# Ordering the taps of a depthwise convolution around a triangular inverse on VectorE

## The chip, the core and the metric

The kernel is one program on one core of a Trainium2 chip. The metric is the device time of one execution in microseconds, the median of several runs. Engines are named as the profile names them: PE (TensorE matmul), PEld (its weight loads), DVE (VectorE), ACT (ScalarE), POOL (GpSimd), SP (SyncE).

## The reference, cut to what matters

The reference runs three transformer-like blocks one after the other on one sequence of 512 tokens with 1024 channels, in fp32. Only the mixing layer of the second block is touched here. It has two branches that meet in one output projection:

```python
y_a = rwkv7_time_mix(...)          # 16 heads of 64; a recurrence over 512 tokens:
#   sa = S @ a_t;  S = S * w_t + sa b_t^T + v_t k_t^T;  y_t = S @ r_t
y_b = conformer_conv(conv_in, ...) # glu = u[:1024] * sigmoid(u[1024:]);
#   z = depthwise causal convolution of glu, 31 taps, 1024 channels, + bias; layer norm; silu
merged = concat([y_a, y_b]) * gates
x = x + gt_m * (merged @ w_out)
```

## The kernel before

Activations lie channel-major, 128 channels by 512 tokens a tile. Each large product is split into three matmuls of a high and a low part (`mm3`, lines 123 to 125); the weights come by DMA on SP's queue and are split by `wsplit` into `whi` (line 117, ACT) and `wlo` (line 118, DVE or POOL).

**The recurrence.** The time mix works on eight pairs of heads, p = 0 to 7, one after the other. For each pair:

- `rwkv_prep` projects r, k and v (matmul, then `shift`, line 1029 on DVE: the tiles `xs_k`, `xs_r`, `xs_v`), normalises k (`kksq` on ACT, the small matmul `ps_kn` on PE, line 1086), makes the products of a chunk with itself (`ps_M`, then `MLR` on DVE, line 1119) and writes the 32 by 32 diagonal blocks to DRAM (`dram_L`).
- `rwkv_invert` reads them back as `uL` (a DMA on ACT's queue), sets the diagonal to one on POOL (line 1161) and inverts the blocks on DVE: 35 small instructions that depend on one another, first a copy of 128x256 into `uM` (line 1177), then multiplies and sums (lines 1171, 1172, 1181 to 1187). The last sum is remembered as `self.inv_last`. The result goes by DRAM into `DT`, and PE finishes it (`ps_D`, `ps_T`, `ps_X`).
- `rwkv_steps` goes through eight chunks of 64 tokens, each a chain PE, DVE and ACT (`zV`, lines 1251 and 1252), PE (`ps_u`), ACT, PE (`ps_s`), DVE (`S`, line 1261). Pair p needs the inverse of p.

**The convolution.** `conv_tiles` makes one or two of the eight tiles of the convolution: a matmul, a gate (`glu`, line 1301 on DVE), a first tap on ACT (line 1303), and then 30 taps on DVE (line 1305), each of which reads and writes the whole tile `z[i]`, so that the taps of one tile form a chain. It is called between the pairs with low priority ("filler"), in the order

```python
order = ["c01", "c12", "c31 g02", "c42", "g22", "c62 g41", ...]
```

where "c12" is `conv_tiles` of two tiles from tile 1 on. List entry 0 is emitted after the inverse of pair 0, entry p + 1 after the inverse of pair p + 1. So the taps of tile 0 are emitted behind inverse 0, those of tiles 1 and 2 behind inverse 1, of tile 3 behind inverse 2, of tiles 4 and 5 behind inverse 3, of tiles 6 and 7 behind inverse 5. Tap 1 of each tile may not be issued before `inv_last` of the inverse that it was emitted behind.

**The order on an engine.** The code is traced once, and a planner fixes at build time in which order each engine issues its instructions: by priority, and by its own notion of when operands are ready. On the chip each engine keeps that order; an instruction that waits holds back all behind it. `issue_after(ins, earlier)` adds an edge for the planner alone, without a semaphore: `ins` stands behind `earlier`.

Of the kernel before, what the change touches and what calls it, by code (L numbers as in the profile page):

```python
# [328 lines left out]
class Block1:  # L329
# [5 lines left out]
    def attend(self, scores, bias, vt, po):  # L335
# [3 lines left out]
        for q0 in (0, 2):  # L339
            PTs = []  # L340
            for e in range(2):
                PT = self.app.tile([128, NB, T // 2], F32, tag="PT", name="PT", bufs=4)
                PTs.append(PT)
                for qb in (q0, q0 + 1):
# [3 lines left out]
                    den = self.sp.tile([128, 1], F32, tag="den", name="den", bufs=6)  # L348
                    p = self.app.tile([128, T], F32, tag="P", name="P", bufs=3)
                    if bias is not None:  # L350
# [240 lines left out]
    def layer1(self):  # L591
# [11 lines left out]
        with ExitStack() as st:  # L603
# [11 lines left out]
            for g0 in range(0, 8, 4):  # L615
                ws = app.tile([128, NB, T // NB], F32, tag="P", name="ws", bufs=3)
                nc.scalar.dma_start(out=ws, in_=a["od_w_s"][0, g0:g0 + 4].rearrange("g i j -> i g j"))
# [80 lines left out]
            for h in range(8):  # L698
# [10 lines left out]
                for cb, s0 in enumerate((0, 8, 24, 32)):  # L709
# [4 lines left out]
                    den = self.sp.tile([128, 1], F32, tag="den", name="den", bufs=6)  # L714
                    p = app.tile([128, 256], F32, tag="P", name="P", bufs=3)
                    nc.vector.tensor_tensor_reduce(out=p, in0=ps[:, 0:256], in1=B[:, (cb + 1) // 2 if cb < 3 else 2].rearrange("p a m -> p (a m)"),
# [33 lines left out]
class Block2:  # L750
# [89 lines left out]
    def block2(self, act, y1):  # L840
        nc, a, tc = self.nc, self.a, self.tc
# [5 lines left out]
        with ExitStack() as st:  # L847
# [158 lines left out]
            order = ["c01", "c12", "c31 g02", "c42", "g22", "c62 g41", "g51 h01", "g62 h13 n h44 x p y04 n2 q r y43 m08 s", "x yw y7 w"]  # L1006
            self.lo_on = "vpp"
            self.n_psp = 0
            P = self.rwkv_prep(W, act, 0, low)
            self.rwkv_invert(P)  # L1010
            for f in order[0].split():
                filler(f)
            for p in range(8):
                low["y7"] = self.rwkv_steps(P, y_d)
                if p < 7:
                    P = self.rwkv_prep(W, act, p + 1, low)
                    self.rwkv_invert(P)
# [131 lines left out]
    def rwkv_invert(self, P):  # L1149


        nc, tc, rp, p = self.nc, self.tc, self.rp, P["p"]
# [10 lines left out]
        M = rp.tile([128, 4, 8, 8], F32, tag="uM", name="uM")  # L1163
        Lf, Mf = L.rearrange("p s t -> p (s t)"), M.rearrange("p g s t -> p (g s t)")

        def prod(out, x, y, dims):

            n = int(np.prod(dims))
            tv = tm[:, 0:n].rearrange({2: "p (a b) -> p a b", 3: "p (a b c) -> p a b c"}[len(dims)],
                                      **dict(zip("bc", dims[1:])))  # L1170
            nc.vector.tensor_tensor(out=tv, in0=x, in1=y, op=ALU.mult)
            self.inv_last = nc.vector.tensor_reduce(out=out, in_=tv, axis=AX.X, op=ALU.add)

        def sub(t, off, *dims):
            return bass.AP(tensor=t.tensor, offset=t.offset + off, ap=[list(t.ap[0])] + [list(x) for x in dims])

        nc.vector.tensor_copy(M, sub(Lf, 0, [264, 4], [32, 8], [1, 8]))
        for (o, n1), (u, su), (v, sv) in (((2, [[1, 2]]), (1, 0), (10, 1)), ((3, [[8, 2]]), (2, 8), (19, 0))):
            tv = tm[:, 0:16].rearrange("p (g b c) -> p g b c", g=4, b=2)
            st = lambda off, s: sub(Mf, off, [64, 4], [36, 2], [s, 2])  # L1180
# [8 lines left out]
        for g in range(4):  # L1189
            w = 8 * g  # L1190
            for j in range(g):
                i0, s0 = 2 * j, 8 * j
                prod(X[:, i0:i0 + 2, w:w + 8], X[:, i0:i0 + 2, s0:w].unsqueeze(2).to_broadcast([128, 2, 8, w - s0]),
                     sub(Lf, 32 * s0 + w, [0, 2], [1, 8], [32, w - s0]), [2, 8, w - s0])
            n = 2 * g + 2
            prod(X[:, 0:n, w:w + 8], X[:, 0:n, w:w + 8].unsqueeze(2).to_broadcast([128, n, 8, 8]),
                 sub(Mf, 64 * g, [0, n], [1, 8], [8, 8]), [n, 8, 8])
        d = tc.dram_tile([16, 2, 8, 4, 32], F32, name=f"dram_DT{p}")
        self.cdma(out=d.rearrange("u b i h t -> h (u b) i t"), in_=X)
        DT = self.zD[p % 2]  # L1200
# [88 lines left out]
    def conv_tiles(self, W, act, c, n, z):  # L1289
        nc, rp = self.nc, self.rp  # L1290
        sg = {}

        def ev(tid, ps):
            kind, i = tid
            if kind == "b":
                g = sg[i] = rp.tile([128, T + 30], F32, tag="glu", name="glu", bufs=3)
                nc.gpsimd.memset(g[:, 0:30], 0.0)
                nc.scalar.activation(out=g[:, 30:], in_=ps, func=AF.Sigmoid)
                return
            g = sg[i]  # L1300
            nc.vector.tensor_tensor(out=g[:, 30:], in0=g[:, 30:], in1=ps, op=ALU.mult)  # L1301
            cw = lambda j: self.col("conv_w_2", j * 8 + i)
            nc.scalar.activation(out=z[i], in_=g[:, 0:T], func=AF.Identity, scale=cw(0), bias=self.col("conv_b_2", i))
            for j in range(1, 31):
                tap = nc.vector.scalar_tensor_tensor(out=z[i], in0=g[:, j:j + T], scalar=cw(j), in1=z[i],  # L1305
                                                     op0=ALU.mult, op1=ALU.add)
                if j == 1:
                    self.issue_after(tap, inv)
            if i == 0:
                self.zsum = self.sp.tile([128, T], F32, tag="ss", name="zs")  # L1310
            elif i == 1:
                nc.gpsimd.tensor_tensor(out=self.zsum, in0=z[0], in1=z[1], op=ALU.add)
            else:
                nc.gpsimd.tensor_tensor(out=self.zsum, in0=self.zsum, in1=z[i], op=ALU.add)

        inv = self.inv_last
        f = 3328 + c * 128
        w = 128 * n
        self.gemm_fm(W, 0, act, [([(f, w), (f + 1024, w)], [(("b", c + i), w + i * 128, 128) for i in range(n)] +
                                  [(("a", c + i), i * 128, 128) for i in range(n)])], ev)  # L1320

    def gate_tiles(self, W, act, g, n, g_d, z=None):
# [555 lines left out]
```

## Time and profile before

| | us |
|---|---|
| median of 3 runs | 3337.91 (3335.11 to 3338.43) |
| the profiled execution, its own time | 3332.78 |
| its span, first to last instruction | 3331.0 |
| PE busy | 3179.2 |
| DVE busy | 2041.3 |
| taps, line 1305, 240 of them | 197.0 |
| stretch of the mixing layer looked at | 1390 to 1980 |

The span is taken by the hardware profiler on the one core. "Idle before" is the time an engine stood still just before an instruction, with the event that ended it. The granted clock is TensorE's, as a share of full speed (2.4 GHz). Matmuls are pipelined and their ends are modelled, so a busy PE is not one at its peak.

### The profile page before, as it was taken

How to read it: one execution, taken by the hardware profiler on the slowest of the kernel's cores; microseconds unless marked ns; L12 is line 12 of the kernel's file. 1: busy time of each engine (PE TensorE's matmuls, PEld its weight loads, DVE VectorE, ACT ScalarE, POOL GpSimd, SP SyncE). 2: the span in 40 equal slices, each digit the busy share in tenths (PEclk: the TensorE clock that was granted, in tenths of full speed). 3: DMA queues.
4: the chain of work that ended last, by engine and by line, in shares of the span. 5: the costliest groups of instructions: out<-in, count | busy, mean ns of one | idle time of the engine just before them, and what ended most of it. 6: DMA issues, size and time to landing. Idle time of an engine off the chain costs nothing. (4 is left out here: it accounts for less than half of the span.)

```text
span 3331.0 us, 43197 instructions
## 1 busy us (share of the span) xinstructions
PE 3179.2 (95%) x15337; PEld 2471.1 (74%) x15337; DVE 2041.3 (61%) x4002; ACT 1386.5 (42%) x2784; POOL 515.1 (15%) x603
## 2 busy tenths in 40 slices
PE   8999999999999999898899889999999999999998
PEld 6755778788778887666666656788877777788887
DVE  4576764654665356688778875434367764575665
ACT  3466332333443233454444444433244553343444
POOL 1000010111211011222223323111010011110111
PEclk9999999999999999999999999999999999999999
DMA  4411553525223332322122343233233125332322
GB/s 134 120 62 50 172 169 128 176 97 149 68 83 95 100 97 76 103 63 68 52 68 66 101 134 113 85 96 95 95 92 112 55 84 164 110 95 95 95 95 82
DMA packets 275032, 332.60 MB, mean 100 GB/s; under 512 B 52956, under 2 KB 188058, under 8 KB 274817
## 3 DMA queue, kind: packets, MB, share of 16 engines
q1 hardware_dynamic: 237392, 301.43, 29.4%
q10 hardware_dynamic: 33489, 12.39, 1.5%
q0 software_dynamic: 3936, 16.03, 1.5%
q8 instruction: 121, 1.98, 0.2%
q14 instruction: 94, 0.77, 0.1%
HBM read 311.88 MB, written 23.89 MB: 101 GB/s over the span
## 5 line engine op out<-in xcount | busy, mean ns | idle before, releaser
L118 DVE TENSOR_TENSOR wlo<-raw,whi 128x512 fp32r<-128x512 f32 (+2 forms) x865 | 625.2, 734 | 752.7 <-PE psg L124 419.3
L123 PE MATMUL psg<-hhi,whi 128*128 128x512 f32 (+1 forms) x2624 | 1044.5, 401 | 36.4 <-DVE glu L1301 7.0
L125 PE MATMUL psg<-hhi,wlo 128*128 128x512 f32 (+1 forms) x2624 | 1038.9, 397 | 13.3 <-DVE wlo L118 7.9
L124 PE MATMUL psg<-hlo,whi 128*128 128x512 f32 (+1 forms) x2624 | 1041.2, 397 | 0.0
L117 ACT CAST whi<-raw 128x512 fp32r<-128x512 f32 (+2 forms) x975 | 581.7, 604 | 1072.6 <-PE psg L124 924.6
L123 PEld LDWEIGHTS psg<-hhi,whi 128*128 128x128 f32 (+1 forms) x2624 | 496.5, 189 | 162.8 <-issue 17.2
L125 PEld LDWEIGHTS psg<-hhi,wlo 128*128 128x128 f32 (+1 forms) x2624 | 496.7, 189 | 124.9 <-POOL wlo L118 9.6
L124 PEld LDWEIGHTS psg<-hlo,whi 128*128 128x128 f32 (+1 forms) x2624 | 497.1, 189 | 107.2 <-issue 7.6
L123 PE MATMUL psg<-hidhi,whi 128*128 128x512 f32 x784 | 308.4, 394 | 1.0 <-DVE ffu L574 0.8
L125 PE MATMUL psg<-hidhi,wlo 128*128 128x512 f32 x784 | 308.0, 393 | 0.0
L124 PE MATMUL psg<-hidlo,whi 128*128 128x512 f32 x784 | 305.9, 390 | 0.0
L1305 DVE SCALAR_TENSOR_TENSOR z<-glu,par_B,z 128x512 f32<-128x512 f32 x240 | 197.0, 835 | 1.5
L118 POOL TENSOR_TENSOR wlo<-raw,whi 128x512 fp32r<-128x512 f32 (+1 forms) x110 | 146.8, 1341 | 281.3 <-ACT whi L117 217.3
L125 PEld LDWEIGHTS psg<-hidhi,wlo 128*128 128x128 f32 x784 | 147.2, 188 | 34.0
L124 PEld LDWEIGHTS psg<-hidlo,whi 128*128 128x128 f32 x784 | 147.2, 188 | 33.4
L123 PEld LDWEIGHTS psg<-hidhi,whi 128*128 128x128 f32 x784 | 147.4, 188 | 32.8 <-DVE ffu L574 1.3
L581 POOL TENSOR_TENSOR ffu<-ffu,ffg 128x512 f32<-128x512 f32 x44 | 64.7, 1469 | 582.6 <-DVE ffu L574 582.6
L1374 POOL TENSOR_TENSOR ffr<-ffr 128x512 f32<-128x512 f32 x32 | 40.1, 1261 | 293.0 <-ACT ffr L1373 286.9
L194 ACT CAST hidhi<-ffu 128x512 fp32r<-128x512 f32 x66 | 41.0, 622 | 106.1 <-POOL ffu L581 66.2
L195 DVE TENSOR_TENSOR hidlo<-ffu,hidhi 128x512 fp32r<-128x512 f32 x66 | 57.3, 868 | 30.9 <-ACT hidhi L194 29.4
L765 DVE SCALAR_TENSOR_TENSOR adacc<-adraw,c_act,adacc 128x1024 f32<-128x1024 f32 x42 | 53.9, 1284 | 33.4 <-DMA adraw<-in_ada_w_dram 33.0
L209 POOL TENSOR_TENSOR ss<-ss,sq 128x512 f32<-128x512 f32 x24 | 35.2, 1467 | 218.1 <-ACT sq L208 202.0
(572 smaller groups left out, 4040.3 us busy)
## 6 DMA issues: line engine op xcount, KB each, us to landing
raw<-in_ffn_w_gu_dram SPq DMA_DIRECT2D x176, 256.0 KB
raw<-in_w_in_dram SPq DMA_DIRECT2D x59, 512.0 KB
adraw<-in_ada_w_dram SPq DMA_DIRECT2D x48, 512.0 KB
raw<-in_w_up_dram SPq DMA_DIRECT2D x88, 256.0 KB
raw<-in_ffn_w_down_dram SPq DMA_DIRECT2D x42, 512.0 KB
raw<-in_w_ff_in_dram SPq DMA_DIRECT2D x32, 512.0 KB
raw<-in_w_ff_out_dram SPq DMA_DIRECT2D x32, 512.0 KB
raw<-in_w_in_dram SPq DMA_DIRECT2D x96, 128.0 KB
```

Source lines behind the costliest of these rows:

```text
L117: nc.scalar.copy(oi(hi), ri(r))
L118: eng.tensor_tensor(out=oi(lo), in0=ri(r), in1=fr(oi(hi)), op=ALU.subtract)
L123: first = nc.tensor.matmul(ps, lhsT=whi, rhs=xhi, start=start, stop=False)
L124: nc.tensor.matmul(ps, lhsT=whi, rhs=xlo, start=False, stop=False)
L125: nc.tensor.matmul(ps, lhsT=wlo, rhs=xhi, start=False, stop=stop)
L194: nc.scalar.copy(hi, t)
L195: nc.vector.tensor_tensor(out=lo, in0=t, in1=fr(hi), op=ALU.subtract)
L209: (nc.gpsimd if c < 4 else nc.vector).tensor_tensor(out=ss, in0=ss, in1=sq, op=ALU.add)
L581: nc.gpsimd.tensor_tensor(out=t, in0=t, in1=part[c], op=ALU.mult)
L765: nc.vector.scalar_tensor_tensor(out=acc, in0=raw, scalar=c[:, k:k + 1], in1=acc, op0=ALU.mult, op1=ALU.add)
L1305: tap = nc.vector.scalar_tensor_tensor(out=z[i], in0=g[:, j:j + T], scalar=cw(j), in1=z[i], op0=ALU.mult, op1=ALU.add)
L1374: nc.gpsimd.tensor_tensor(out=t, in0=t, in1=t, op=ALU.mult)
```

## The change

Each `conv_tiles` call now notes its taps in a list, `self.taps`, in the order in which they are emitted: the 30 of its first tile, then the 30 of its second if there is one. The next inverse takes the list. With k half its length, but at most 20, the inverse's first instruction (the copy into `uM`) is placed behind tap k, and tap k + 1 (counted from one) is placed behind the inverse's last sum. Then the list is emptied. Tile 0's 30 taps give k = 15 at inverse 1; tiles 1 and 2 give k = 20 at inverse 2; tile 3 gives 15 at inverse 3; tiles 4 and 5 give 20 at inverse 4; tiles 6 and 7 give 20 at inverse 6. Inverses 0, 5 and 7 find an empty list. No instruction is added or removed, and no semaphore wait.

```diff
@@ in block2
             self.n_psp = 0
+            self.taps = []
             P = self.rwkv_prep(W, act, 0, low)
@@ in rwkv_invert
-        nc.vector.tensor_copy(M, sub(Lf, 0, [264, 4], [32, 8], [1, 8]))
+        first = nc.vector.tensor_copy(M, sub(Lf, 0, [264, 4], [32, 8], [1, 8]))
...
+        if self.taps:
+            k = min(len(self.taps) // 2, 20)
+            self.issue_after(first, self.taps[k - 1])
+            self.issue_after(self.taps[k], self.inv_last)
+        self.taps = []
         d = tc.dram_tile([16, 2, 8, 4, 32], F32, name=f"dram_DT{p}")
@@ in conv_tiles
                 if j == 1:
                     self.issue_after(tap, inv)
+                self.taps.append(tap)
```

## Rows read from the trace of the kernel before

**Rows 1.** The page's busy time by engine: us, share of the span, instructions.
```profile
PE 3179.2 (95%) x15337; PEld 2471.1 (74%) x15337; DVE 2041.3 (61%) x4002; ACT 1386.5 (42%) x2784; POOL 515.1 (15%) x603
```

**Rows 2.** Stretches: length, busy PE, PEld, DVE, ACT, POOL (instructions), clock, DMA share, GB/s.
```profile
1390.00:1980.00 590.00, 521.21 (x3246) 378.07 (x3245) 484.77 (x1034) 274.12 (x709) 163.36 (x199) 0.95 0.28 78
1537.70:1578.00 40.30, 33.91 (x156) 25.63 (x156) 37.87 (x88) 20.85 (x53) 13.97 (x17) 0.92 0.25 78
1578.00:1627.60 49.60, 41.94 (x302) 29.74 (x300) 36.77 (x59) 19.47 (x45) 11.62 (x17) 0.97 0.18 44
1627.60:1667.30 39.70, 32.02 (x142) 23.13 (x143) 33.75 (x86) 18.52 (x51) 11.03 (x13) 0.84 0.20 57
1667.30:1714.90 47.60, 45.62 (x328) 33.24 (x326) 34.05 (x64) 21.28 (x52) 13.04 (x17) 0.99 0.27 70
1714.90:1753.50 38.60, 33.35 (x158) 24.53 (x158) 33.96 (x92) 20.67 (x57) 11.21 (x13) 0.87 0.20 60
```

**Rows 3.** Taps alone, line 1305, by stretch: length, DVE busy (taps), clock, DMA.
```profile
1410.70:1457.40 46.70, 21.15 (x25) 1.00 0.27 69
1457.40:1480.45 23.05, 3.69 (x5) 1.00 0.23 66
1480.45:1537.70 57.25, 26.07 (x35) 0.94 0.24 65
1537.70:1578.00 40.30, 15.68 (x17) 0.92 0.25 78
1578.00:1627.60 49.60, 23.64 (x26) 0.97 0.18 44
1627.60:1667.30 39.70, 10.17 (x12) 0.84 0.20 57
1667.30:1714.90 47.60, 21.87 (x28) 0.99 0.27 70
1714.90:1753.50 38.60, 6.65 (x9) 0.87 0.20 60
1869.50:1907.05 37.55, 7.84 (x10) 1.00 0.24 71
```

**Rows 4.** Timeline of PE: start, us, instruction, idle before it and its releaser.
```profile
1485.36 0.50 PE L123 MATMUL psg<-hhi,whi 128*128 128x512 f32 x1 [0.96 <-DVE xs_k L1029]
1488.64 1.05 PE L1086 MATMUL ps_kn<-bones,kksq 128*128 128x2 f32 x8 [1.84 <-ACT kksq L1083]
1631.55 0.80 PE L123 MATMUL psg<-hhi,whi 128*128 128x512 f32 x1 [4.64 <-DVE glu L1301]
1661.43 1.87 PE L1086 MATMUL ps_kn<-bones,kksq 128*128 128x2 f32 x8 [3.63 <-ACT kksq L1083]
1716.54 0.69 PE L1255 MATMUL ps_u<-zV,zD 128*64 128x128 f32 x2 [2.67 <-ACT zV L1252]
```

**Rows 5.** Stretches behind the PE stall at 1661, columns as in rows 2.
```profile
1661.40:1665.00 3.60, 3.57 (x12) 3.20 (x13) 3.33 (x15) 2.42 (x4) 0.20 (x2) 0.50 0.38 109
1665.00:1668.50 3.50, 3.50 (x10) 2.76 (x9) 3.50 (x8) 1.11 (x4) 0.52 (x1) 0.54 0.00 0
```

**Rows 6.** Timeline of DVE: two taps in a row, six in a row, inverse starts.
```profile
1434.90 1.52 DVE L1305 SCALAR_TENSOR_TENSOR z<-glu,par_B,z 128x512 f32<-128x512 f32 x2
1523.61 4.05 DVE L1305 SCALAR_TENSOR_TENSOR z<-glu,par_B,z 128x512 f32<-128x512 f32 x6
1627.61 0.29 DVE L1177 COPY uM<-uL 128x256 f32<-128x256 f32 x1 [4.43 <-POOL uL L1161]
1659.31 0.74 DVE L1029 SCALAR_TENSOR_TENSOR xs_k<-psg,mu,pp 128x512 f32<-128x512 f32 x1
1714.99 0.29 DVE L1177 COPY uM<-uL 128x256 f32<-128x256 f32 x1 [5.53 <-POOL uL L1161]
1715.98 0.22 DVE L1251 COPY zV<-ps_v 64x64 f32<-64x64 f32 x1
```

**Rows 7.** Timeline of POOL: the sum of tiles 0 and 1, columns as in rows 4.
```profile
1550.18 1.53 POOL L1312 TENSOR_TENSOR zs<-z,z 128x512 f32<-128x512 f32 x1 [0.38 <-DVE z L1305]
```

## The prediction

> **What bounds the kernel now.** I read the busy time by engine first: PE is busy for 95% of the span, DVE for 61% [rows 1]. A change that only moves DVE work can give time back only where PE stands still or runs at its lower clock. So I read next the stretch in which the taps lie. From 1390 to 1980, 590 us, PE is busy for 521.2 us [rows 2]: 68.8 us are idle, and the mean granted clock is 0.95, so that some 0.05 x 590 = 29 us more go to the lower clock. Those 98 us are all that any reordering here could return; a good part of them belongs to waits that have nothing to do with taps.
>
> Then I cut this stretch at the starts and ends of the inverses. While an inverse runs, DVE is nearly full and PE is not: 37.9 of 40.3 us and 33.9 us in inverse 2, 33.8 of 39.7 and 32.0 in inverse 3, 34.0 of 38.6 and 33.4 in inverse 4, at a clock of 0.92, 0.84 and 0.87 [rows 2]. Between the inverses it is the other way round: behind inverse 3, PE is busy for 45.6 of 47.6 us at 0.99 and DVE for only 34.0 [rows 2]. So DVE time is dear inside an inverse and cheap outside.
>
> How many taps lie inside? 5 in inverse 1, 17 in inverse 2, 12 in inverse 3, 9 in inverse 4, 10 in inverse 6 [rows 3]: 53 in all. The last view is the list of PE's stalls. In inverse 3 PE waits 3.63 us for `kksq`, which ACT makes from `xs_k`; DVE wrote `xs_k` at 1659.31 without any idle time before it [rows 4, 6], so it was late because of what stood ahead of it on DVE. Two other stalls, 4.64 us for `glu` at 1631 and 2.67 us for `zV` at 1716 [rows 4], stand right behind an inverse's first instruction, which had held DVE for 4.43 and 5.53 us until POOL had finished `uL` [rows 6]. Taps do not cause these two.
>
> **The change part by part.** Nothing is added or removed; the planner gets two edges at each of five inverses. They name DVE instructions only: no DMA issue is moved past another, and the write of the inverse's result stands behind the last sum as before.
>
> *Price of a tap.* Two taps of one chain in a row take 1.52 us, 0.76 each. Six in a row in the stretch before inverse 2 take 4.05 us, 0.675 each [rows 6]; there two tiles are at work, and I read the shorter step as taps of the two in turn. So a tap costs DVE 0.675 to 0.76 us wherever it stands.
>
> *Single tiles, inverses 1 and 3.* Both edges hold the whole tile: 15 taps before, 15 behind. The 12 taps of inverse 3 go behind it, 12 x 0.675 to 0.76 = 8.1 to 9.1 us of DVE. Even if only half of them stood ahead of `xs_k`, 6 x 0.675 = 4.1 us is more than the stall of 3.63 us, so I take that stall as gone. It costs more than itself: behind it the granted clock is 0.50 for 3.6 us and 0.54 for 3.5 us [rows 5], a loss of 3.6 x 0.50 + 3.5 x 0.46 = 3.4 us. Inverse 3 thus gives 3.63 + 3.4 = 7.0 us. Inverse 1 loses 5 taps, 3.4 to 3.8 us; behind it PE waits 0.96 us for `xs_k` and 1.84 us for `kksq` [rows 4], 2.8 us. But 10 of the 25 taps that stood before inverse 1 [rows 3], and the 5 inside, now follow right behind it, where `xs_k` is made. Between 0 and 2.8 us I take the middle, 1.4 us.
>
> *Two tiles, inverses 2, 4 and 6.* Here the edges do less than they say. Tap 21 of the first tile waits for the inverse, and with it taps 22 to 30, its chain. The second tile's taps have no edge: they need only their own chain and the inverse that they were emitted behind. The trace shows that the planner does run two tiles at once: 25 + 5 + 35 = 65 taps had run before inverse 2 began [rows 3], more than the 60 of tiles 0 and 1, and yet POOL, which adds these two tiles, still waited for a tap until 1550.2, inside the inverse [rows 7]. So the second tile can fill the gaps of the inverse as the first did. I expect inverse 2 to keep 10 to 17 taps, inverse 4 some 9, inverse 6 some 10, and I count their gain as 0; all out would be at most (17 + 9 + 10) x 0.76 = 27 us of DVE.
>
> *Where the moved taps go.* Behind inverse 3, DVE has 47.6 - 34.05 = 13.5 us free [rows 2], enough for 15 taps at 0.76, 11.4 us. That cover is what makes them free; without it, the 27 taps that now follow their own predecessor (15 and 12) would cost 27 x (0.76 - 0.675) = 2.3 us more than where they stood in turn. I take 0. The Trainium skill, "VectorE: DVE Perf Modes", section "The DRAIN you can't avoid", states that eight copies with a semaphore after each take as long as eight with one at the end, so that a chain costs nothing over independent work. By that rule the 2.3 us would be 0 and a tap would cost the same in either place. The trace disagrees: 0.76 against 0.675 us [rows 6].
>
> *What waits behind the new edges.* The inverse's first instruction now stands behind tap 15 or 20. It has DMA data to wait for anyway, 4.43 us at inverse 3 and 5.53 us at inverse 4 [rows 6], so that six or seven taps fit there unpaid. Behind it on DVE stand the `zV` copies of the recurrence, on which PE waits. If the planner, seeing the first instruction later, puts `glu` and `zV` ahead of it, the stalls of 4.64 and 2.67 us [rows 4] go as well, 7.3 us; if not, they stay. I take 0 and keep 7.3 us for the range.
>
> **The sum.** 7.0 + 1.4 = 8.4 us. The profiled execution took 3332.8 us; less 8.4 that is 3324.4 us. It was 5.1 us under the median of the runs, so on the scale of the median the forecast is 3337.9 - 8.4 = 3329.5 us, with its own range from 3337.9 - 8.4 - 7.3 = 3322 us to 3331 us, where it stops being faster.
>
> **The rivals.**
>
> *The taps only change places.* PE keeps its order and its filler matmuls; behind inverse 3 it was busy for 45.6 of 47.6 us [rows 2], so the inverse's result was not awaited there. If `xs_k` is late again because other work takes the freed slots, the time stays, 3338 us within 6.7 us. For it: 36 of the 53 taps can stay inside through the second tile. Against it: inverse 3 holds single-tile taps only.
>
> *The forced taps hold up the inverse: slower.* The 15 taps put behind inverse 1 push the others back. Before inverse 2, 35 slots were used [rows 3]; 15 now go to tile 0, 20 are left for tiles 1 and 2, and the first needs 20: up to 10 missing, 7.6 us. Before inverse 4, 28 slots [rows 3], 15 for tile 3, 13 for two tiles: 7 to 13 missing, 5.3 to 9.9 us, less the wait of 5.5 us. Before inverse 3 the leftovers of tiles 1 and 2, some 18, take most of the 26 slots: 7 missing, 5.3 us, less 4.4 us. Together up to 7.6 + 4.4 + 0.9 = 13 us of later inverses, and the last tile is done about 10 us later, in front of the layer norm. It decides as soon as the taps still missing, at 0.76 us, outlast the wait for `uL`. I put 10 us: 3348 us. For it: these waits are the only slack that the rows show. Against: PE has filler work meanwhile.
>
> *All taps stay out.* If the planner does hold the second tiles back too, 53 x 0.675 = 36 us of DVE leave the inverses. PE's idle time in inverses 2, 3 and 4 is 6.4 + 7.7 + 5.2 = 19.3 us, and the clock costs 0.08 x 40.3 + 0.16 x 39.7 + 0.13 x 38.6 = 14.6 us [rows 2]; two thirds of these 33.9 us are 22.6 us: 3315 us. Against it: no edge holds the second tile.
>
> **How the numbers follow.** 0.2% of the time, 6.7 us, is about what a measurement of this kernel can tell from no change. The forecast gets 0.33, all taps out 0.12, changed places 0.30, forced taps 0.25. Faster is then 0.45, the same 0.30, slower 0.25. For 8 in 10 the range goes from 3312 us, a little beyond the 3315 of all taps out, to 3351 us, the full 13 us of the forced taps, and leaves out what lies further on either side.
>
> **What would show it.** Right: no tap inside inverses 1 and 3, inverse 3 shorter by 6 to 9 us, the stall of 3.63 us for `kksq` gone, the clock in inverse 3 up from 0.84; at least 8 taps each still inside inverses 2 and 4. Wrong, if inverses 2, 4 and 6 are empty (all taps out), or if the first instructions of inverses 2 to 4 no longer wait for `uL` and start later (forced taps), or if PE's idle time over the stretch stays near 69 us with other stalls in place of these (changed places).

## The result: slower by 38 us

The changed kernel takes 3375.98 us, the median of four executions (3375.46 to 3380.83); beside it the kernel before took 3338.12 us. The ratio is 1.0119, 95% interval 1.0101 to 1.0136: **slower by 1.2%**. The forecast was 3329.5 us, and the range ended at 3351 us. The profiled execution took 3380.83 us; in it the recurrence begins some 4 us later than in that of before, so 4 us are to be taken off its positions.

The page's busy time by engine, of the kernel after (columns as in [rows 1]):

```profile
PE 3195.1 (95%) x15337; PEld 2483.1 (73%) x15337; DVE 2047.9 (61%) x4002; ACT 1390.3 (41%) x2785; POOL 509.1 (15%) x603
```

The span grew from 3331.0 to 3379.0 us, by 48.0. PE's busy time grew by 15.9 us [rows 1], for the same 15337 matmuls at a lower granted clock (0.974 in the mean of the execution, against 0.983), and its idle time by 32.1. ACT's one instruction more is a load of an activation table, 1.28 us; all other runs below have as many of them as the kernel before, so it is not the cause. (The two profiled executions lie on opposite sides of their medians, so they differ by 10 us more than these.) Of the 48 us, 4.3 lie ahead of the recurrence, 34.1 in it and 9.6 behind it. Here are the stretch from the chunk products (`MLR`) of pair 0 to the last chunk of pair 7, of before and then of after, and further rows of after (columns as in [rows 2]):

```profile
1375.90:2040.10 664.20, 586.40 (x3655) 423.40 (x3656) 526.17 (x1125) 318.57 (x810) 187.33 (x218) 0.95 0.29 82
```

```profile
1380.20:2078.50 698.30, 591.97 (x3622) 427.83 (x3623) 527.95 (x1120) 321.37 (x808) 180.00 (x216) 0.91 0.27 77
...
1461.90:1480.30 18.40, 16.60 (x89) 11.82 (x90) 17.52 (x46) 11.31 (x29) 4.50 (x7) 1.00 0.09 25
1550.50:1590.60 40.10, 33.93 (x141) 25.52 (x141) 35.50 (x84) 21.07 (x54) 11.98 (x13) 0.79 0.23 73
1616.60:1655.00 38.40, 36.75 (x222) 25.37 (x223) 24.13 (x50) 22.54 (x64) 10.93 (x14) 1.00 0.19 51
1655.00:1678.80 23.80, 19.28 (x78) 15.16 (x77) 23.35 (x60) 11.86 (x24) 5.96 (x8) 0.88 0.35 105
1743.50:1781.70 38.20, 31.86 (x152) 25.04 (x152) 36.07 (x82) 16.17 (x40) 12.04 (x9) 0.91 0.17 51
```

The stretch is 34.1 us longer: PE's idle time went from 664.20 - 586.40 = 77.8 to 698.30 - 591.97 = 106.3 us, 28.5 more, and 5.6 us went to PE's busy time, at a mean granted clock of 0.91 instead of 0.95. DVE has nearly the same to do in both (526 and 528 us). Inverse 1 (second row of after) shrank from 23.0 to 18.4 us, inverse 3 (fifth) from 39.7 to 23.8 us [rows 2, 3]. Yet the whole is slower. The fourth row is the time between `MLR` of pair 3 and the start of its inverse: 38.4 us, where it had been 18.0.

The taps alone, by stretch, of after (line 1311; columns as in [rows 3]):

```profile
1414.90:1461.80 46.90, 13.06 (x15) 1.00 0.28 68
1461.80:1480.30 18.50, 0.17 (x1) 1.00 0.09 25
1480.30:1550.50 70.20, 34.34 (x41) 0.95 0.26 68
1550.50:1590.60 40.10, 13.99 (x16) 0.79 0.23 73
1590.60:1655.00 64.40, 25.05 (x33) 0.89 0.15 39
1655.00:1678.80 23.80, 0.14 (x1) 0.88 0.35 105
1678.80:1743.50 64.70, 30.17 (x39) 0.99 0.25 69
1743.50:1781.70 38.20, 13.22 (x17) 0.91 0.17 51
1886.10:1927.30 41.20, 8.36 (x12) 0.92 0.19 57
```

Inverses 1 and 3 hold only the edge of one tap each; 2, 4 and 6 show 16, 17 and 12, a tap at an edge counted in. The edges did to the taps what the prediction said they would. Inverse 5, which has no edge and is in no count so far, went from 6 taps to 19.

The timeline of PE, its larger stalls, of after (columns as in [rows 4]):

```profile
1495.95 0.79 PE L123 MATMUL psg<-hhi,whi 128*128 128x512 f32 x1 [6.19 <-DVE xs_k L1030]
...
1552.19 0.69 PE L1261 MATMUL ps_u<-zV,zD 128*64 128x128 f32 x2 [4.35 <-ACT zV L1258]
...
1672.83 1.76 PE L1087 MATMUL ps_kn<-bones,kksq 128*128 128x2 f32 x8 [2.65 <-ACT kksq L1084]
...
1792.50 1.09 PE L1217 MATMUL ps_D<-ident,zD 128*128 128x128 f32 x4 [7.32 <-DMA zD<-dram_DT]
```

The stalls of 4.64 us for `glu` and 2.67 us for `zV` [rows 4] are not there, and that for `kksq` in inverse 3 is 2.65 us instead of 3.63 (third row). Others are new, at other places.

### The profile page after: what moved, and what is told of

It reads as the page before. It is cut to its first block, busy times and chain, and to the rows that moved or that the text cites. A ratio compares the mean times of both kernels' runs of the same rounds, so it can differ in the third digit from the quotient of the medians.

```text
span 3379.0 us, 43211 instructions
## 1 busy us (share of the span) xinstructions
PE 3195.1 (95%) x15337; PEld 2483.1 (73%) x15337; DVE 2047.9 (61%) x4002; ACT 1390.3 (41%) x2785; POOL 509.1 (15%) x603
## 5 line engine op out<-in xcount | busy, mean ns | idle before, releaser
L123 PEld LDWEIGHTS psg<-hidhi,whi 128*128 128x128 f32 x784 | 147.4, 188 | 34.1 <-issue 1.6
```

What stands on the lines that cost most here:

```text
L123: first = nc.tensor.matmul(ps, lhsT=whi, rhs=xhi, start=start, stop=False)
```

## The experiments

Eighteen kernels, each set against the kernel before on the same chip. The first four take the change apart. Their expectations name theories by letters: A lays the loss on both edges together (the back edge stores up taps, and the front edge makes the next inverse wait for them), B on the front edges alone, C on a new order as such, D on the back edges, which push taps into the stretches behind. Later D1 is that last theory for the taps of tile 0, D2 one of a DMA wait on ACT, and O the new order of all other work.

**1. Front edges alone, back edges alone.** Each run leaves out one of the two lines:

```diff
-            self.issue_after(first, self.taps[k - 1])      # left out in the second run
-            self.issue_after(self.taps[k], self.inv_last)  # left out in the first run
```

> The front edge alone (the inverse behind tap 15 or 20), at all five inverses, the back edge left out. Theory A, that it takes both edges (the back edge stores up a backlog, the front edge then makes the inverse wait for it): the built order puts 25, 35, 26, 32 and 41 taps before inverses 1, 2, 3, 4 and 6, almost as before, so 3338 us within 7. Theory B, that the front edge is enough to hold the inverse up: slower by 20 us or more, 3358 to 3380. Theory C, that any new edge throws the planner's order about: 20 us or more either way.

> The back edge alone (the rest of the first tile behind the inverse), at all five inverses, the front edge left out. Theory A: no inverse waits for taps, so inverse 3 starts as long behind its MLR as before (18 us, against 38 us with the change) and inverse 4 as before (20 us, against 38): 3330 to 3346 us. Theory B (the front edge alone): the same here, 3330 to 3346. A third theory, D, that the taps pushed back are the cost wherever they run (they meet the recurrence's DVE work): slower by 20 us or more, 3358 to 3380, with inverses that start on time.

Front alone: 3342.4 us, ratio 1.0017 [1.0006, 1.0027]. Back alone: 3367.61 us, 1.0089 [1.0072, 1.0106]. In the second, inverse 3 starts 19 us behind its `MLR`, as before, and 31 of the 38 us are lost all the same. So A and B don't explain most of it; the second run is what D forecast.

**2. Both edges at inverse 3 alone, and at all but inverse 1.**

```diff
-        if self.taps:
+        if self.taps and p == 3:     # second run: p > 1
```

> Both edges at inverse 3 alone. There is no backlog from inverse 1; 26 slots before inverse 3 hold the 8 left over and 15 of tile 3. Theory A: inverse 3 starts about 20 us behind its MLR as before, is empty of taps and some 15 us shorter (24 instead of 40 us, as with the change), 3326 to 3340 us. Theory B or D: slower by 5 to 20 us, 3343 to 3358.

> Both edges at inverses 2, 3, 4 and 6, none at inverse 1: the 15 taps of tile 0 are not stored up, but 10 of tile 1 and 15 of tile 3 are, and inverses 2 to 4 still wait for 20, 15 and 20 taps. Theory A with the backlog from inverse 1 as its main part: most of the loss goes, 3338 to 3352 us. Theory A with the later edges (tile 3 before inverse 3, the backlog of tile 3 before inverse 4) as its main part: most of the loss stays, 3358 to 3380 us, and the first instructions of inverses 3 and 4 start 35 us or more behind their MLR.

3342.09 us, 1.0022 [1.0011, 1.0032], and 3346.0 us, 1.0027 [1.0015, 1.0039]. In the first, inverse 3 takes 20.6 us instead of 39.7 [rows 2], and nothing is gained. Without the edges at inverse 1 there is little loss.

**3. The edges at inverse 1 alone; the same with 25 taps in front, as before; the change with a DMA order; no taps.** With inverse 1 empty of taps, ACT's queue had the read of its result (`zD<-dram_DT`) among the squares of the group norm, and waited. The timeline of ACT and then of DVE, of the kernel after:

```profile
1487.64 0.35 ACT L1279 ACTIVATE ysq<-Y,gn_m 128x64 f32<-128x64 f32 x1 [4.54 <-DMA dram_DT<-uX]
```

```profile
1488.11 0.17 DVE L1280 TENSOR_SCALAR gn_v<-gn_v 128x8 f32<-128x8 f32 x1 [1.87 <-ACT ysq L1279]
...
1495.16 0.74 DVE L1030 SCALAR_TENSOR_TENSOR xs_k<-psg,mu,pp 128x512 f32<-128x512 f32 x1
```

The square waits 4.54 us for the landing, `gn_v` for the square, `xs_k` stands behind both on DVE, and PE waits 6.19 us for it (above). That made theory D2. But DVE itself stood still for only 1.87 us, and between `gn_v` and `xs_k` it ran five taps of tile 0, 0.75 + 1.79 + 1.82 + 0.74 + 0.74 = 5.84 us, which the back edge had pushed there. So these rows alone fit D1 as well. The edits:

```diff
+        if self.taps and p == 1:                        # runs 1 and 2
+            k = 25                                      # run 2 only
...
+                if p: self.issue_after(rd, self.gn_sq)  # run 3, beside the whole change:
+                                                        # the reads behind the last square
...
-            for j in range(1, 31):                      # run 4, without any edge
+            for j in range(1, 2):
```

> Both edges at inverse 1 alone: 15 taps of tile 0 in front of it, 15 behind, the other inverses without edges. Theory D1 (taps pushed back): the 10 taps that had free slots in front of inverse 1 are stored and fall into the stretch before inverse 2, where room is short; this run is then about as slow as the back edges everywhere, 3355 to 3368 us. Theory D2 (ScalarE's order of issue): with inverse 1 empty of taps it ends about 5 us earlier in the plan, and its result's DMA write and reads are placed on ScalarE ahead of squares of the group norm of steps 0; ScalarE waits there for a landing, and xs_k and PE with it, a stall of about 6 us behind inverse 1 and steps 1 some 10 us late: 3345 to 3358 us. If inverse 1 is not the place of the loss: within 6 us of before, 3331 to 3344 us.

> Edges at inverse 1 alone, with 25 taps of tile 0 in front, as the kernel before has them, and only the 5 that lay inside put behind. Theory D1 (taps pushed back): nothing is pushed back but 5 taps, 3.8 us of VectorE, so within 6 us of before, 3331 to 3344 us, and no stall of 6 us for xs_k. Theory D2 (ScalarE's order): inverse 1 is as empty as in the change, the landing is awaited on ScalarE in front of the group norm here too, so a stall of several us for xs_k behind inverse 1 and a time close to that of the edges at inverse 1 with 15 taps in front, within 5 us of it.

> The change as it is, with one edge more: the reads of the inverse's result from DRAM (from inverse 1 on) are issued on ScalarE behind the last square of the group norm that was built before them, so that no square waits for a landing. Theory D2: the 6 us stall for xs_k behind inverse 1 goes to under 3 us, steps 1 end 6 to 10 us earlier than in the change, and the time falls by 8 to 20 us, to 3355 to 3368 us; inverses 3 and 4 are still held up by their front edges. Theory D1: the order of these issues costs nothing, the stall is moved only, and the time stays within 6 us of the changed kernel, 3370 to 3382 us.

> Leaves out 29 of the 30 taps of each tile (only tap 1 is kept), so the convolution is incomplete; no edges at the inverses. It bounds what taps in the inverses can cost at all: 8 x 29 = 232 taps, 157 to 176 us of VectorE, are gone from the stretch. If the prediction's price holds (taps in the inverses delay PE), PE's 69 us of idle time and the 29 us of lower clock fall by at least the 22 us reckoned for all taps out, and the time is 3315 us or less. If VectorE's taps are not what PE waits for in the stretch, the time is within 10 us of before, 3328 to 3348 us.

| run | median, us | ratio to before |
|---|---|---|
| edges at inverse 1 alone | 3369.35 | 1.0098 [1.0083, 1.0113] |
| the same, 25 taps in front | 3356.55 | 1.0059 [1.0042, 1.0076] |
| the change, reads behind the squares | 3350.54 | 1.0038 [1.0023, 1.0053] |
| 29 of 30 taps of each tile left out | 3339.16 | 1.0005 [0.9995, 1.0014] |

Inverse 1 alone costs 32 of the 38 us, and moving five taps costs 19. Neither theory is borne out: the second run lies between D1's range (no loss) and D2's (within 5 us of the first), and the third gained more than D2 forecast, which D1 did not expect at all. The last row shows what leaving nearly all taps out brings. Three stretches of the kernel without taps, its inverses 2, 3 and 4 (columns as in [rows 2]), and its whole recurrence:

```profile
1536.90:1557.20 20.30, 19.09 (x108) 13.13 (x108) 16.95 (x49) 8.72 (x30) 2.74 (x4) 0.92 0.11 35
1612.50:1629.60 17.10, 15.73 (x89) 11.85 (x90) 15.93 (x42) 10.98 (x32) 4.26 (x6) 1.00 0.09 26
1701.60:1718.00 16.40, 10.23 (x27) 7.41 (x28) 15.85 (x51) 7.24 (x15) 2.10 (x2) 0.51 0.22 74
```

```profile
1378.80:2028.40 649.60, 571.20 (x3608) 412.27 (x3608) 360.86 (x884) 312.55 (x799) 169.29 (x212) 0.94 0.29 82
```

These inverses take half the time and DVE has 165 us less to do, but PE stands still for 649.60 - 571.20 = 78.4 us, against 77.8. The stretch is 14.6 us shorter and holds 15.2 us less PE work, which comes after it instead. So leaving the taps out returned nothing. The planner laid out the order of this run anew too, though, so it does not by itself part the price of the taps from that of a new order; the fourth run of part 5, in the old order, bears on that.

**4. D2 by itself, in four ways.** The cure with the edges at inverse 1; the cure without front edges; the cure alone; and the wait alone, put into the kernel before:

```diff
+        if p == 1: self.issue_after(wr, self.gn_sq)      # run 1: the DMA write behind the last square
...
+                if p: self.issue_after(rd, self.gn_sq)   # runs 2 and 3: the reads behind it
...
+                if p == 1 and e + blk == 0:              # run 4: the last square behind a read
+                    self.issue_after(self.gn_sq, rd)
```

> Both edges at inverse 1 alone, with 15 taps in front as in the change, and one edge more: ScalarE issues the DMA write of inverse 1's result behind the last square of the group norm of steps 0, so that neither write nor reads stand in front of a square. Theory D2 (the squares wait on ScalarE for write and landing): the whole 32 us that the edges at inverse 1 cost go, apart from replanning: 3335 to 3347 us, no stall over 3 us for xs_k behind inverse 1. Theory D1 (10 taps stored into the next stretch, which cost there): at least half of the 32 us stays, 3353 us or more. By the run with 25 taps in front and 5 behind (19 us slower, against 32) both may hold a share: then 3345 to 3353 us.

> The change without its front edges, with the back edges at all five inverses, and with the reads of the inverse's result issued on ScalarE behind the group norm's squares. The change with that order took 3350.5 us. If the 13 us that are left there come from inverses 3 and 4 that wait for their forced taps (theory B), they start 15 to 20 us earlier without front edges, and the time falls to 3336 to 3344 us. If they come from the taps pushed back (theory D1), it stays at 3347 to 3355 us.

> The kernel before with the order of the reads behind the group norm's squares alone, no edge on taps: the control for that edge. In the kernel before the reads of inverse 1 stand behind the squares already, so nothing changes up to inverse 6: all theories expect the time of before within 6 us, 3331 to 3344 us. A gain of over 10 us here would mean that the edge itself, and not the cure of the change's wait, gave the 25 us.

> The suspected wait alone, put into the kernel before: no edge on taps; the last square of the group norm of steps 0 is issued on ScalarE behind the first read of inverse 1's result, so that it waits for the landing of the write. Taps lie as before up to inverse 2. Theory D2: ScalarE waits some 4 us at that square, xs_k of the next stretch comes late, PE stalls some 5 us for it, and the time is 5 to 20 us above before, 3343 to 3358 us. Theory D1: taps were the cause, so this wait is absorbed: 3331 to 3342 us.

| run | median, us | ratio to before |
|---|---|---|
| edges at inverse 1, write and reads behind the squares | 3375.61 | 1.0115 [1.0097, 1.0132] |
| back edges everywhere, reads behind the squares | 3343.87 | 1.0015 [1.0004, 1.0027] |
| reads behind the squares, no edge on taps | 3342.67 | 1.0018 [1.0009, 1.0028] |
| the wait alone | 3339.6 | 1.001 [1.0, 1.0019] |

D2 falls as the main cause, by the first run. The last run, with the wait alone, does not test it. The wait is there on ACT, and the run is 3.6 us slower, hardly clear of noise (the interval begins at 1.0). But the planner put `gn_v` behind `xs_k`, so that `xs_k` does not stand behind the wait, and PE waits only 0.66 us for it. The timelines of ACT and of DVE in that run:

```profile
1493.72 0.35 ACT L1277 ACTIVATE ysq<-Y,gn_m 128x64 f32<-128x64 f32 x1 [3.26 <-DMA dram_DT<-uX]
```

```profile
1492.77 0.74 DVE L1030 SCALAR_TENSOR_TENSOR xs_k<-psg,mu,pp 128x512 f32<-128x512 f32 x1
...
1494.19 0.18 DVE L1278 TENSOR_SCALAR gn_v<-gn_v 128x8 f32<-128x8 f32 x1
```

Taken out where only inverse 1 has edges, the wait returns nothing (as D1 forecast): there steps 1 end 166.1 us behind `MLR` of pair 0, against 171.6 in the kernel before, as theory D2 has it, but `MLR` of pair 4 comes 16.2 us and the end of steps 7 37.2 us later than before, in pairs that have no edge. One extra edge moved the time by some 25 us in the change and by some 24 us without front edges, and by next to nothing or in the wrong direction elsewhere. The second run also lies in the range that theory B named for it, 7 us under the same change with its front edges (3350.54 us), with intervals that overlap. That speaks for theory O: any edge makes the planner lay out everything behind it anew.

**5. Place of the taps against order of all else.** A chain of edges can hold an engine to a given order. In the traces of the three runs below that are held to the old order, PE's and ACT's instructions over the recurrence stand as in the kernel before, and DVE's too but for the taps. So each can be changed alone:

```diff
+PIN = """
...
+"""
...
+            made = {i.name: i for i in nc.cur_bb.bb.instructions}
+            last = {}
+            for n in PIN.split():          # some 6,200 instructions in the order of a build, taps moved
+                i = made["I-" + n]
+                if i.engine in last:
+                    tc.add_manual_dep(i, last[i.engine], ..., reason="pin")
+                last[i.engine] = i.name
```

> The order of the kernel before is pinned on TensorE, ScalarE and SyncE, instruction by instruction, and on VectorE for all but the taps; only the taps of tile 0 lie as the edges at inverse 1 put them (15 in front, none inside, 15 behind), with GpSimd's sums and the clearing of the next buffer following them. If the place of the taps is what costs, as theory D1 says, this run is as slow as the one with the edges at inverse 1 alone (3369 us): 3360 to 3375 us. If the loss lies in the order that the planner laid out anew for all the other work (theory O), the taps cost nothing here: 3331 to 3344 us. The prediction's own figure for inverse 1, 1.4 us, would be within that.

> The counterpart: the order that the planner laid out for the edges at inverse 1 alone is pinned on TensorE, ScalarE and SyncE, and on VectorE for all but the taps of tile 0, which go back to where the kernel before has them (25 in front of inverse 1, 5 inside); no edges. Theory D1: with the taps back it is as fast as before, 3331 to 3344 us. Theory O: it stays as slow as with the edges, 3362 to 3375 us.

> The order of before pinned as above; only the 12 taps of tile 3 inside inverse 3 are put behind it, one behind each second other instruction of VectorE from the eighth on. The prediction's step for inverse 3: the stall of 3.63 us for kksq and the slow clock behind it go, 7.0 us: 3327 to 3332 us. If the time that inverse 3 gives back is spent later, as the runs with edges there and without any taps (3339 us) say: within 3 us of before, 3334 to 3340 us.

> The order of before pinned as above; all 43 taps inside inverses 1 to 4 are put behind their inverses, spread between the other instructions of VectorE. The prediction's rival of all taps out reckoned 22 us for these places together (with inverse 6): 3313 to 3322 us. If the inverse's length is not what TensorE waits for over the stretch: 3330 to 3340 us. If taps spread behind the inverses stand in front of other work that is awaited there: above 3344 us.

| order of PE, ACT, SP and the rest of DVE | taps of tile 0 as before | as the edges put them |
|---|---|---|
| as before | 1 (the kernel before, 3337.15 us) | 1.0020 [1.0010, 1.0030] (3343.88 us) |
| as laid out for the edges at inverse 1 | 1.0122 [1.0108, 1.0135] (3376.67 us) | 1.0098 [1.0083, 1.0113] (3369.35 us) |

Read down the columns, the order costs 3376.67 - 3337.15 = 39.5 us with the taps in their old places and 3369.35 - 3343.88 = 25.5 us with the taps moved (these two come from different sets of runs; by their ratios it is 26). Read along the rows, the place of the taps costs 6.7 us in the old order and gives 7.3 us back in the new one, where the two intervals overlap. Theory O holds, and for the taps of tile 0 theory D1 falls but for those 6.7 us. The taps of the other tiles keep their new places in the second run (21 in inverse 3, where the kernel before has 12), so what D1 would make of them is part of "the order" here; part 6 bears on it.

A place where such a loss can be seen is the one where the prediction looked for a gain. In the first run no square of the group norm waits for a landing, the taps stand ahead of `xs_k`, and PE waits 5.89 us for it, against 0.96 us before [rows 4]. The timeline of PE:

```profile
1492.30 0.79 PE L123 MATMUL psg<-hhi,whi 128*128 128x512 f32 x1 [5.89 <-DVE xs_k L1029]
```

Taps out of inverse 3 in the old order: 3338.66 us, 1.0003 [0.9994, 1.0012]. Taps out of inverses 1 to 4: 3345.25 us, 1.0022 [1.0011, 1.0033], the third reading of its expectation. Here is inverse 3 of the first, and PE's stall in it:

```profile
1632.10:1667.40 35.30, 30.38 (x146) 22.06 (x147) 23.96 (x74) 19.19 (x54) 9.10 (x12) 0.90 0.22 64
```

```profile
1661.77 1.05 PE L1086 MATMUL ps_kn<-bones,kksq 128*128 128x2 f32 x8 [2.35 <-ACT kksq L1083]
```

Twelve taps are gone, DVE's busy time fell from 33.75 to 23.96 us [rows 2], but the inverse only from 39.7 to 35.3: with PE's order unchanged, DVE now waits. The stall for `kksq` went from 3.63 to 2.35 us [rows 4], not to 0. In the kernel before the last tap ahead of `xs_k` had ended at 1651.6, 7.7 us before `xs_k` began, and DVE stood still 0.46 us for ACT in between: the taps were not all that it waited for.

**6. TensorE's order alone.** The same pin on PE only, once to take the new order out of the change, once to put it into the kernel before:

> The change with all its edges, and TensorE's order pinned to that of the kernel before, instruction by instruction over the stretch of the recurrence; the planner is free on all other engines. If it is TensorE's new order that costs, most of the 38 us come back: 3335 to 3350 us. If the new orders of VectorE and ScalarE, or the front edges that hold inverses 3 and 4, cost without it too, 3355 to 3376 us.

> No edge on taps; TensorE's order alone is pinned to the one that the planner laid out for the edges at inverse 1 alone, and the planner is free on all other engines. If TensorE's order alone carries the loss: 3360 to 3380 us. If it costs only together with the other engines' orders, which the planner can fit to it here: 3335 to 3352 us.

The change with PE's old order: 3359.93 us, 1.0078 [1.0055, 1.0102]. PE's new order without any edge on taps: 3386.73 us, 1.0154 [1.0136, 1.0173]. Both miss the range that stood for PE's order alone: keeping the old one returns 16 of the change's 38 us, which is the second reading's range, and the new one alone costs 49 us, 10 more than all new orders together in part 5. In the second run here the other engines were laid out anew around it, so a part of the 49 us may be that they do not fit PE's order. The place of the taps is not what the three kernels with this order of PE share: edges at inverse 1, the second run of part 5 and this one hold 21, 21 and 1 taps in inverse 3 and 13, 13 and 2 in inverse 4, and lose 32, 39.5 and 49 us. Of the 22 us that remain in the first run, with PE's old order, a part can be read in its timeline of PE:

```profile
1589.38 0.80 PE L123 MATMUL psg<-hhi,whi 128*128 128x512 f32 x1 [9.28 <-DVE glu L1307]
...
1965.01 1.72 PE L272 MATMUL ps_bc<-diag,ones 128*128 128x512 f32 x2 [11.90 <-DVE diag L270]
```

DVE is still free to be laid out anew there, and PE, held to the old order, meets it late.

**What the new order does** can be seen in the second run of part 5 (taps of tile 0 back in their old places, new order). Its recurrence, columns as in [rows 2], to be set against the first row of before in the section on the result:

```profile
1377.50:2080.90 703.40, 603.70 (x3658) 434.75 (x3659) 529.45 (x1126) 320.92 (x811) 188.38 (x218) 0.92 0.27 78
```

It is 703.40 - 664.20 = 39.2 us longer, the whole loss. PE stands still for 703.40 - 603.70 = 99.7 us, 21.9 more; the other 17.3 us are busy time of PE, for three matmuls more, at a mean granted clock of 0.92 instead of 0.95. So nearly half of the loss is the lower clock and not a wait. Groups of PE's instructions over the whole recurrence: line, tile, shapes, count, busy us, mean ns, idle before them and what ended it; first of the kernel before, then of that run:

```profile
L125 PE MATMUL psg<-hhi,wlo 128*128 128x512 f32 x409 | 171.5, 426 | 12.3 <-DVE wlo L118 7.9 <-POOL wlo L118 3.9 <-POOL pp L1027 0.3
L1255 PE MATMUL ps_u<-zV,zD 128*64 128x128 f32 x128 | 28.7, 307 | 18.7 <-ACT zV L1252 18.6
L1248 PE MATMUL ps_v<-VU,MLR 128*64 128x64 f32 x256 | 23.2, 247 | 1.9 <-DVE S L1261 1.7
...
L1281 PE MATMUL ps_yt<-ident,Y 128*128 128x128 f32 x28 | 9.1, 326 | 1.6 <-ACT Y L1278 1.6
```

```profile
L125 PE MATMUL psg<-hhi,wlo 128*128 128x512 f32 x409 | 175.1, 436 | 22.2 <-POOL wlo L118 12.1 <-DVE wlo L118 10.1
L1261 PE MATMUL ps_u<-zV,zD 128*64 128x128 f32 x128 | 29.3, 313 | 8.7 <-ACT zV L1258 8.6
L1254 PE MATMUL ps_v<-VU,MLR 128*64 128x64 f32 x256 | 23.7, 250 | 15.9 <-DVE S L1267 15.9
...
L1287 PE MATMUL ps_yt<-ident,Y 128*128 128x128 f32 x28 | 8.9, 317 | 7.5 <-ACT Y L1284 7.5
```

Waits for `zV` fall by 10.0 us; those for `S`, `Y` and `wlo` rise by 14.0 + 5.9 + 9.9 = 29.8; smaller groups make up the rest of the 21.9. One place of it, the start of inverse 3 in the timeline of DVE and what PE makes of it:

```profile
1635.92 0.29 DVE L1178 COPY uM<-uL 128x256 f32<-128x256 f32 x1 [5.20 <-POOL uL L1162]
...
1637.14 0.57 DVE L1267 SCALAR_TENSOR_TENSOR S<-S,GC,ps_s 64x64 f32<-64x64 f32 x2
```

```profile
1637.85 0.34 PE L1254 MATMUL ps_v<-VU,MLR 128*64 128x64 f32 x4 [3.54 <-DVE S L1267]
...
1660.25 0.48 PE L1287 MATMUL ps_yt<-ident,Y 128*128 128x128 f32 x1 [6.97 <-ACT Y L1284]
```

The inverse's first copy holds DVE for 5.20 us until its data is there, as it held it for 4.43 us in the kernel before [rows 6]. Before, `glu` stood behind it, and PE waited 4.64 us for that [rows 4]; in the new order the recurrence's `S` does, and PE waits 3.54 us. So this wait only changed its cause. The next one is new: the group norm of pair 2 runs in between the instructions of the inverse, as it did before, but PE now reaches the transposes of `Y` 6.97 us too early, at 1660.25; in the kernel before it came to them at 1669.04 and did not wait.

## Why the prediction was wrong

- **The step that failed** is the first line of the change part by part, "Nothing is added or removed; the planner gets two edges", together with the rival's "PE keeps its order and its filler matmuls". All steps after it move taps within an order that stays. The planner lays out all engines anew behind an edge; that order, laid out for the edges at inverse 1 and put in with the taps of tile 0 in their old places, costs 39.5 us. In the whole change, PE's old order returns 16 of the 38 us.
- **"DVE time is dear inside an inverse"** was read from busy shares, and no run bears it out: without 29 of 30 taps inverses 2 to 4 take 16 to 20 us and the time stays, 1.0005 [0.9995, 1.0014], if in an order laid out anew; with the 43 taps moved out in the old order it is 8 us longer. So the 98 us of idle time and lower clock were not the taps' to give back: in the run without taps PE stands still as long as before over the recurrence (78.4 and 77.8 us).
- **Inverse 3, 7.0 us**: 0, by the run that moves its 12 taps and nothing else (1.0003 [0.9994, 1.0012]). The stall for `kksq` kept 2.35 of 3.63 us. DVE was not late by the taps alone: 9.8 us less work shortened the inverse by 4.4 us.
- **Inverse 1, 1.4 us, and the moved taps free**: the place of the taps of tile 0 alone costs 6.7 us, not a gain. The prediction saw that the taps would follow where `xs_k` is made, but let them take back no more than the 2.8 us; PE's wait for `xs_k` grew to 5.89 us. The cover behind the inverse was not complete.
- **Price of a tap, 0.675 to 0.76 us wherever it stands**: too low by the prediction's own rows. [rows 3] give 15.68 us for 17 taps in inverse 2, 0.92 each, and the table of the kernel before gives 197.0 us for all 240, 0.82 each.
- **"Taps do not cause these two"**, the stalls for `glu` and `zV`: in part they do. Between the inverse's first copy and `glu` stood two taps of 1.48 and 0.73 us in the kernel before, and one of 0.75 us ahead of `zV`.
- **Two tiles, inverses 2, 4 and 6**: right that they keep their taps. 16, 17 and 12 stayed, against 10 to 17, some 9 and some 10; inverse 4 holds nearly twice its figure.
- **The rival "forced taps hold up the inverse"** has the sign, and a part of its mechanism: inverse 3 starts 38.4 us behind `MLR` instead of 18.0, without waiting for `uL`, and inverse 4 likewise. But it was priced at 10 us and would have to explain 38, and the back edges alone, which force nothing in front, lose 31.
- **The rival "all taps stay out", 3315 us**: neither run with empty inverses gained. The one in the old order moves the taps and the one without taps is laid out anew; taps left out in the old order were not tried.
- Of the Trainium skill's rule, the section "The DRAIN you can't avoid" of "VectorE: DVE Perf Modes", nothing was decided on the time: 2.3 us and 0 cannot be told apart here. The section measures copies with and without semaphores; that a chain costs nothing beside independent work is the prediction's reading of it.

What stays open: which part of PE's new order costs and why the clock is lower in it, whether the order of the whole change costs as much as that for inverse 1 (only PE's was taken out there), and how the 22 us that remain with PE's old order divide between DVE's and ACT's orders and the inverses held up by their forced taps. Whether PE's old order would be as good with other work beside it was not tried.

## What to carry to other kernels

Where a planner orders all engines at build time, an edge on one engine is an edit of the whole order: compare the built orders of the other engines before you cost the edge itself, and if you want to know what the moved work costs, hold everything else to the old order. Before you cost a relief, leave the work out altogether, and hold the order of the rest while you do: if the time does not fall then, the waits are somewhere else. None of the twelve kernels here that the planner laid out anew without a pin was faster than before (ratios from 1.0005 to 1.0115); whether another kernel would lose as well was not tried.

## What the hardware showed that was not expected

- An instruction on DVE runs longer beside a tensor operation on GpSimd. In the kernel after, behind inverse 1, two taps took 1.79 and 1.82 us where others there take 0.74, and a small 128x8 product 1.22 where it otherwise takes 0.15, while GpSimd made three `wlo`. The timelines of DVE and of POOL:

```profile
1489.00 1.79 DVE L1311 SCALAR_TENSOR_TENSOR z<-glu,par_B,z 128x512 f32<-128x512 f32 x1
1490.71 1.22 DVE L254 TENSOR_TENSOR rs_t<-rs_y 128x8 f32<-128x8 f32 x1
1491.86 1.82 DVE L1311 SCALAR_TENSOR_TENSOR z<-glu,par_B,z 128x512 f32<-128x512 f32 x1
...
1493.68 0.74 DVE L1311 SCALAR_TENSOR_TENSOR z<-glu,par_B,z 128x512 f32<-128x512 f32 x1
```

```profile
1488.96 4.17 POOL L118 TENSOR_TENSOR wlo<-raw,whi 128x512 fp32r<-128x512 f32 x3 [0.75 <-PE psg L125]
```

  So the price of a tap, read from two places as 0.675 to 0.76 us, depends on what GpSimd does meanwhile. In the trace of the kernel before, the 176 taps beside which GpSimd runs no tensor operation take 0.742 us in the mean and at most 0.78; the other 64 take 1.09 us in the mean and up to 2.4, and every tap over 1 us is among them. That is read from the traces, and no run here tested it alone. The Trainium skill, "SBUF — State Buffer", section "SBUF: two separate sides", states an exclusive lock on a shared pair of ports, for which an operation of VectorE with two inputs in SBUF and one of GpSimd that reads SBUF exclude each other for a whole instruction. A tap has two such inputs, and these rows agree with it.
- A DMA issue that waits in ACT's queue holds the arithmetic behind it: 4.54 us for one landing. Whether PE feels it depends on what stands behind: with a wait of 3.26 us put into the kernel before, `xs_k` did not hang on it, and the time differed by 3.6 us, hardly clear of noise.
